# The down projection of a ConvFFN block: 16 of its 22 blocks of weights as seven products instead of eight

## The chip, the cores and the metric

The kernel runs on one core of a Trainium2 chip. The metric is the device time of the whole launch in microseconds. TensorE is PE in the profile (PEld is its loading of the stationary operand), VectorE is DVE, ScalarE is ACT, GpSimd is POOL and SyncE is SP.

## The reference

One decoder block on x of 512 tokens x 1024 channels, in float32. Two token mixers (a causal convolution and an HGRN2 recurrence) are merged by gates, projected, and added to the residual:

```
x = layer_norm(ALPHA * x + mix, ln1_g, ln1_b)
z = x @ w_ffn_in                                   # 1024 -> 2 * 2816
u, gv = split(z);  u = causal_dwconv(u, w_ffn_dw, b_ffn_dw)      # 3 taps
y_ffn = (gelu(u) * gv) @ w_ffn_out                 # 2816 -> 1024
x = layer_norm(ALPHA * x + y_ffn, ln2_g, ln2_b)
```

## The kernel before

Every product is made of three matmuls (mm3): both operands are split into a high part, the float32r cast, and a low part, the rest, and hi x hi, hi x lo and lo x hi are summed in PSUM. Weights lie in DRAM as tiles of 128 x 1024 floats (512 KB). `fetch(i)` loads one on SP's queue into a raw buffer (three of them), casts the high part on ScalarE and subtracts for the low part on VectorE; high and low parts have a ring of five buffers each. `weight(i)` fetches up to three tiles ahead.

The stages, in order: input projections and mixers (to about 400 us); the output projection with the first layer norm (437 to 482 us), whose result goes to DRAM as x1_d and, transposed and split, to x1h and x1l; the up projection; the down projection with the second layer norm.

The up projection has 22 blocks of 128 hidden channels. Blocks 0 to 2 are plain. Blocks 3 to 21 each replace eight half-size products by seven (`seven_up`, `seven`): `weight_sums` builds sums of quarters of a block's weights on VectorE, `factor_sums` once builds sums of the activations, and each block runs b11, b21, t1, t2, b22, t3 and then t4, which is held back as `pending` and runs inside the next block. `act` makes the hidden tile hT[j]. A block is 7 x 4 x 3 = 84 matmuls of 256 columns. Sums of the block ahead are prepared while a block runs.

The down projection is plain before: for 16 blocks, each weight tile is used for four token blocks and two column halves, so 24 matmuls of 512 columns for one tile; hidden(k) splits hT[k]. The last six blocks run token block by token block, so that the layer norm of one overlaps the matmuls of the next. In the first of the 16 blocks VectorE also multiplies x1a (the residual, read back from x1_d in one load of 2 MB) with the first layer norm's gain and adds its bias; gains and biases of both norms come as lnp, one broadcast load of 2 MB on POOL's queue.

The order within each engine's queue is made by a planner: it takes the program's order as priority, follows dependencies and buffers, and simulates with its own costs. A tile with the same tag as an older one takes that one's place once all its readers are done.

Of the kernel before, what the change touches and what calls it, by code (L numbers as in the profile page):

```python
# [13 lines left out]
PLAIN = 3  # L14
# [47 lines left out]


@with_exitstack
def hybrid_block(ctx: ExitStack, tc: tile.TileContext, wts: bass.AP, xT_d: bass.AP,
# [29 lines left out]
    def limit(i):  # L95
        return min(e for e in (W_G, W_FI + 2 * PLAIN, W_N) if e > i) - 1
# [14 lines left out]
    resident = {}  # L111

    def fetch(i):
        raw = wp.tile([P, 1024], F32, tag="raw", name=f"wr{i}", bufs=3)
        parts = 4 if i == 0 else 1
        n = 1024 // parts
        pieces = [slice(j * n, j * n + n) for j in range(parts)]
        for c in pieces:
            nc.sync.dma_start(raw[:, c], wts[i][:, c])
# [78 lines left out]

    pads = [p1p.tile([P, 64], F32, name="pad0")]
# [383 lines left out]
    def weight_sums(i, t, b21, extra):  # L583
# [210 lines left out]
    x1_d = ctx.enter_context(tc.tile_pool(name="dram", bufs=1, space=bass.MemoryType.DRAM)).tile([T, D], F32, name="x1_d")  # L794
# [28 lines left out]
    keep = {}  # L823

# [30 lines left out]
    for half in range(2):  # L855
# [22 lines left out]
    NK = 16  # L878
    hT = {}

    def hid():

        for tag, c0, n in [("ch", 0, 4), ("cl", 4, 4)] + [(f"sc{i}", 8 + 2 * i, 2) for i in range(4)]:
# [3 lines left out]
        for c in range(16, NFF):  # L887
            hT[c] = tmp.tile([P, T], F32, tag=("tot", "kt", "gg")[(c - 16) // 2], name=f"hT{c}")
# [40 lines left out]
    def prepare(j):  # L929
# [22 lines left out]
    hid()  # L952
# [16 lines left out]
    lnp = p1p.tile([P, 4, 1024], F32, tag="xl", name="lnp")  # L969
    po.dma_start(lnp, ln_d.unsqueeze(0).broadcast_to([P, 4, 1024]))  # L970
    bks = [4, 5, 0, 1, 2, 3, 6, 7]
    yps = {}

    res = p1p.tile([P, 4, 1024], F32R, tag="xh", name="fores")
    resident[W_FO + NK] = lambda: (res[:, 0], res[:, 1])
    resident[W_FO + NK + 1] = lambda: (res[:, 2], res[:, 3])
    x1a = p1p.tile([P, NT, 1024], F32, tag="ol", name="x1a")
    nc.sync.dma_start(x1a, x1_d.rearrange("(b p) c -> p b c", p=P))
    hres = [p1p.tile([P, 2, T], F32R, tag=f"sv{i}", name=f"hres{i}") for i in range(4)]
    hsp = {}  # L980

    def hidden(k):

        if k not in hsp:
            if NK <= k < NK + 4:
                hi, lo = hres[k - NK][:, 0], hres[k - NK][:, 1]
            else:
                if k % 2:
                    hl = tmp.tile([P, 2, T], F32R, tag="qq", name=f"hq{k}")
                    hi, lo = hl[:, 0], hl[:, 1]  # L990
                else:
                    hi, lo = [tmp.tile([P, T], F32R, tag=t, name=f"h{t}{k}") for t in ("kT", "t1")]
            split(hi, lo, hT[k])
            hsp[k] = (hi, lo)
        return hsp[k]
# [24 lines left out]
    ws = [weight(W_FO + k) for k in range(NK, NFF)]  # L1020
    for k in range(NK, NFF):
        hidden(k)
    for tb in range(NT):
        for n in range(2):
            for k in range(NK, NFF):
                down(k, ws[k - NK], tb, (n,))
# [4 lines left out]
        for n, c in enumerate(halves):  # L1031
            ve.scalar_tensor_tensor(x1a[:, tb, c], x1a[:, tb, c], ALPHA, yps[tb][n], ALU.mult, ALU.add)
# [9 lines left out]
def pack(inp):  # L1042
# [27 lines left out]
    tiles.append(f("w_ffn_out")[0].reshape(NFF, P, 1024))  # L1070
# [40 lines left out]
```

## Time and profile before

| | |
|---|---|
| Time, median of 3 runs | 840.9 us (840.44 to 841.75) |
| The profiled execution | 840.79 us, of which 839.0 us is the span of the trace |
| PE busy | 821.0 us, 98% |
| VectorE busy | 617.0 us, 74% |
| ScalarE busy | 460.6 us, 55% |
| DMA moved | 113.40 MB |

The span runs from the first to the last event of the trace on the core. PE's busy time is modelled, since matmuls overlap; whether PE waits is read from the chain of waits and from the start times of matmuls.

### The profile page before, as it was taken

What the parts mean: (1) busy time and instruction counts of PE and PEld (TensorE: products, weight loads), DVE (VectorE), ACT (ScalarE), POOL (GpSimd) and SP (SyncE); (2) the same over time, 40 slices, a digit from 0 to 9 for tenths busy, and PEclk for the clock granted to TensorE, in tenths of its full rate; (3) what the DMA queues carried; (4) which work ended last, traced back from release to release, by engine and by line L of the source; (5) the groups of instructions that cost most, each with busy time, mean ns of one, the idle gap of its engine ahead of it and who ended that gap; (6) DMA issues with size and microseconds to landing.
All of it is one profiled execution on the core that took longest, in us unless ns stands there. A gap on an engine that the chain in (4) does not pass through costs nothing.

```text
span 839.0 us, 14550 instructions
## 1 busy us (share of the span) xinstructions
PE 821.0 (98%) x5771; PEld 719.7 (86%) x5771; DVE 617.0 (74%) x1113; ACT 460.6 (55%) x820; POOL 87.8 (10%) x147
## 2 busy tenths in 40 slices
PE   8999999999999999999999999999999999999995
PEld 6888778777777778999978899999999999888884
DVE  5369999955587638788474689689998999844356
ACT  4455555667678865566641556566666666423200
POOL 0112431433332400000100000000000000000000
PEclk9999999999999999999999999999999999999998
DMA  8688666654543664233675332323333234634101
GB/s 287 177 180 206 167 148 155 166 135 128 130 126 98 170 171 138 76 104 110 162 242 187 115 113 76 95 84 104 118 106 101 101 102 161 271 121 130 46 26 75
DMA packets 32995, 113.40 MB, mean 135 GB/s; under 512 B 3616, under 2 KB 4512, under 8 KB 32800
## 3 DMA queue, kind: packets, MB, share of 16 engines
q1 hardware_dynamic: 24288, 82.85, 29.6%
q0 software_dynamic: 6480, 25.17, 14.9%
q10 hardware_dynamic: 2160, 4.47, 1.5%
q8 instruction: 45, 0.74, 0.4%
q14 instruction: 22, 0.18, 0.1%
HBM read 85.21 MB, written 4.19 MB: 107 GB/s over the span
## 4 chain that ended last, share of the span: by engine, by line
PE 78%; DVE 12%; ACT 4%; DMA 3%; issue 1%; DVEq 0%; ACTq 0%; POOLq 0%; SPq 0%
PE ps L159 25%; PE ps L160 24%; PE ps L161 24%; DVE cws L262 6%; DMA wr<-in_wts 2%; DMA xr<-in_xT 1%; PE ps L379 1%; ACT wh L127 1%; PE ps L528 1%; DVE tt L412 1%; PE ps L530 1%; PE ps L543 1%; DMA wl<-wr 1%; PE ps L517 1%; PE ps L492 0%
## 5 line engine op out<-in xcount | busy, mean ns | idle before, releaser
L159 PE MATMUL ps<-xh,wh 128*128 128x512 f32 x256 | 104.4, 409 | 0.5 <-ACT xh L152 0.4
L160 PE MATMUL ps<-xl,wh 128*128 128x512 f32 x256 | 100.9, 394 | 0.5 <-DVE xl L155 0.5
L161 PE MATMUL ps<-xh,wl 128*128 128x512 f32 x256 | 100.4, 392 | 0.0
L262 DVE SCALAR_TENSOR_TENSOR cws<-cws,par 128x512 f32<-128x512 f32 x120 | 84.8, 756 | 0.1
L140 ACT CAST wh<-wr 128x1024 fp32r<-128x1024 f32 x34 | 35.6, 1049 | 61.3 <-PE ps L161 34.3
L141 DVE TENSOR_TENSOR wl<-wr,wh 128x1024 fp32r<-128x1024 f32 (+1 forms) x38 | 43.2, 1139 | 34.7 <-ACT wh L140 34.4
L127 ACT CAST wh<-wr 128x1024 fp32r<-128x1024 f32 x44 | 46.4, 1057 | 39.1 <-PE ps L160 27.8
L159 PE MATMUL ps<-sh,shi_t 128*128 128x256 f32 x228 | 64.5, 283 | 0.0
L160 PE MATMUL ps<-sl,shi_t 128*128 128x256 f32 x228 | 64.5, 283 | 0.0
L161 PE MATMUL ps<-sh,slo_t 128*128 128x256 f32 x228 | 64.5, 283 | 0.0
L129 POOL DMA_DIRECT2D wl<-wr x44 | 38.6, 877 | 225.4 <-ACT wl L128 205.3
L159 PEld LDWEIGHTS ps<-xh,wh 128*128 128x128 f32 x256 | 48.2, 188 | 12.0 <-ACT xh L152 1.9
L161 PEld LDWEIGHTS ps<-xh,wl 128*128 128x128 f32 x256 | 48.1, 188 | 10.2
L160 PEld LDWEIGHTS ps<-xl,wh 128*128 128x128 f32 x256 | 48.2, 188 | 9.8 <-DVE xl L155 1.2
L155 DVE TENSOR_TENSOR slo_t<-Toh,shi_t 128x1024 fp32r<-128x1024 f32 x38 | 46.4, 1221 | 12.6 <-ACT shi_t L152 11.9
L152 ACT CAST shi_t<-Toh 128x1024 fp32r<-128x1024 f32 x38 | 39.9, 1050 | 16.7 <-PE ps L160 8.3
L128 ACT ACTIVATE wl<-wh 128x1024 fp32r<-128x1024 f32 x44 | 46.6, 1059 | 0.8
L159 PEld LDWEIGHTS ps<-sh,shi_t 128*128 128x128 f32 x228 | 43.8, 192 | 0.0
L160 PEld LDWEIGHTS ps<-sl,shi_t 128*128 128x128 f32 x228 | 43.8, 192 | 0.0
L161 PEld LDWEIGHTS ps<-sh,slo_t 128*128 128x128 f32 x228 | 43.8, 192 | 0.0
L568 ACT COPY pc<-ps 128x256 f32<-128x256 f32 x57 | 21.2, 372 | 37.0 <-PE ps L161 36.8
L155 DVE TENSOR_TENSOR slo_b<-wr,shi_b 128x1024 fp32r<-128x1024 f32 x27 | 32.9, 1218 | 2.4 <-ACT shi_b L152 2.4
(384 smaller groups left out, 2552.4 us busy)
## 6 DMA issues: line engine op xcount, KB each, us to landing
wr<-in_wts SPq DMA_DIRECT2D x141, 512.0 KB, 3.8
wl<-wr POOLq DMA_DIRECT2D x44, 512.0 KB, 4.9
xr<-in_xT ACTq DMA_DIRECT2D x8, 256.0 KB, 5.2
x<-in_x ACTq DMA_DIRECT2D x4, 512.0 KB, 9.9
x_d<-x SPq DMA_DIRECT2D x4, 512.0 KB, 4.1
x1a<-x_d SPq DMA_DIRECT2D x1, 2048.0 KB, 8.4
lnp<-in_ln POOLq DMA_DIRECT2D x1, 2048.0 KB, 10.6
out<-x1a SPq DMA_DIRECT2D x8, 256.0 KB, 2.0
```

The lines of the kernel that those rows point to most:

```text
L127: ac.copy(hi, raw)
L128: ac.mul(lo, hi, -1.0)
L129: po.dma_start(lo, raw, accum_op=ALU.add)
L140: ac.copy(hi[:, c], raw[:, c])
L141: ve.tensor_tensor(lo[:, c], raw[:, c], hi[:, c], ALU.subtract)
L152: ac.copy(hi, src)
L155: (lo_eng or ve).tensor_tensor(lo, src, hi, ALU.subtract)
L159: pe.matmul(ps, a[0], b[0], start=start, stop=False, skip_group_check=more)
L160: pe.matmul(ps, a[0], b[1], start=False, stop=False, skip_group_check=more)
L161: pe.matmul(ps, a[1], b[0], start=False, stop=stop, skip_group_check=more)
L262: ve.scalar_tensor_tensor(cacc[j], cpad[j][:, i:i + T], w, cacc[j], ALU.mult, ALU.add)
L568: f(*args)
```

## The change

The first 16 blocks of hidden channels (2048 of 2816) are treated as one 2 x 2 problem: tokens in halves of 256, hidden channels in halves of 1024, output columns in halves of 512. Seven products replace eight, in the order b11, t1, t2, b22, t3, b21, t4; each has four weight tiles of 128 x 1024 (two hidden blocks by 512 columns), repacked on the host. The operand of each product is made on VectorE from quarters of hT (`operand`): four sums for t1, t2, b22 and t3, and four splits for all seven.

The sums t1 to t4 of the weights are not built on VectorE. `fo_sums(j)` issues for blocks 4 to 19 of the up projection, on POOL's queue, a 64-byte store of a piece of hT[j-2] into the target (it holds the rest back until hT[j-2] exists), then a copy of 512 KB from DRAM to DRAM, then a DMA of 512 KB that accumulates into it. The down projection then loads 28 + 6 tiles instead of 22.

The products go into PSUM banks named X, W, Z and V, a pair of each. Four partial sums are read out into x1a between products (`take_sum`, after b11, t1, t2 and t3), and X and Z go on accumulating.

The first norm's gain and bias on the residual move from the down projection to the output projection (`residual`, for token blocks 0 and 1 among the second half's matmuls, for 2 and 3 after block 3 of the up projection has been prepared); the store to x1_d follows it. gb1 and gb2, two broadcast tiles each of 512 KB, replace lnp. x1a takes the place of x1l instead of that of the activation sums. The scratch tiles of `weight_sums` swap places with its spare ring entries (oh0, oh1 against oh2, oh3). There are four raw weight buffers instead of three; two pad tiles go and four convolution tiles get 64 floats shorter.

```diff
+FOP = ("b11", "t1", "t2", "b22", "t3", "b21", "t4")
+FO_OF = {"b11": 0, "b21": 4, "b22": 8, "b12": 12}
+NK = 16
+W_S = W_FO + 4 * len(FOP) + 6
...
+    tsum = {t: [dp.tile([P, 1024], F32, name=f"{t}_{m}") for m in range(4)] for t in ("t1", "t2", "t3", "t4")}
+
+    def source(i):
+        if i < W_FO:
+            return wts[i]
+        n = i - W_FO
+        if n >= 4 * len(FOP):
+            return wts[W_FO + NK + n - 4 * len(FOP)]
+        t, m = FOP[n // 4], n % 4
+        return wts[W_FO + FO_OF[t] + m] if t in FO_OF else tsum[t][m]
...
-        raw = wp.tile([P, 1024], F32, tag="raw", name=f"wr{i}", bufs=3)
+        raw = wp.tile([P, 1024], F32, tag="raw", name=f"wr{i}", bufs=4)
...
-    pads = [p1p.tile([P, 64], F32, name="pad0")]
...
-    cws = [p1p.tile([P, 1152], F32, tag=f"sc{j}", name=f"cws{j}") for j in range(4)]
+    cws = [p1p.tile([P, 1088], F32, tag=f"sc{j}", name=f"cws{j}") for j in range(4)]
...
+    gb1 = [p1p.tile([P, 1024], F32, tag=f"sc{2 + i}", name=f"gb1_{i}") for i in range(2)]
+    for i in range(2):
+        ac.dma_start(gb1[i], ln_d[i:i + 1].broadcast_to([P, 1024]))
+
+    def residual(tb):
+        ve.tensor_tensor(x1[tb], x1[tb], gb1[0], ALU.mult)
+        ve.tensor_tensor(x1[tb], x1[tb], gb1[1], ALU.add)
+        nc.sync.dma_start(x1_d[tb * P:tb * P + P, :], x1[tb])
...
-            nc.sync.dma_start(x1_d[tb * P:tb * P + P, :], x1[tb])
...
+            (late if half else steps).append(lambda tb=tb: residual(tb))
...
-        t = [p1p.tile([P, 1024], F32, tag=tag, name=f"T{tag}_{j}") for tag in ("oh2", "oh3")]
+        t = [p1p.tile([P, 1024], F32, tag=tag, name=f"T{tag}_{j}") for tag in ("oh0", "oh1")]
...
-        return weight_sums(i, t, b21, ("oh0", "oh1"))
+        return weight_sums(i, t, b21, ("oh2", "oh3"))
...
+    def fo_sums(j):
+
+        fo = lambda t, m: wts[W_FO + FO_OF[t] + m]
+        m, c = divmod(j - NF - 1, 4)
+        if 0 <= m < 4:
+            t, b, a = (("t1", "b12", fo("b11", m)), ("t3", "b12", fo("b22", m)), ("t2", "b22", tsum["t1"][m]),
+                       ("t4", "b21", tsum["t2"][m]))[c]
+
+            po.dma_start(tsum[t][m][0:1, 0:16], hT[j - 2][0:1, 0:16])
+            po.dma_start(tsum[t][m], fo(b, m))
+            po.dma_start(tsum[t][m], a, accum_op=ALU.add, max_dma_last_dim=4096)
+
     for j in range(NF, NFF):
+        fo_sums(j)
         if j == NF:
             w = prepare(j)
+            for f in late:
+                f()
+            hid(1)
...
-    lnp = p1p.tile([P, 4, 1024], F32, tag="xl", name="lnp")
-    po.dma_start(lnp, ln_d.unsqueeze(0).broadcast_to([P, 4, 1024]))
...
-    x1a = p1p.tile([P, NT, 1024], F32, tag="ol", name="x1a")
+    x1a = p1p.tile([P, NT, 1024], F32, tag="xl", name="x1a")
...
+    def operand(t):
+
+        out = []
+        for q in range(4):
+            g = lambda a: halfT[a, q]
+            if t == "t1":
+                src = s12[q]
+                ve.tensor_tensor(src, g("a21"), g("a22"), ALU.subtract)
...
+            else:
+                src = g({"b11": "a11", "b21": "a12", "t4": "a22"}[t])
+            o = homes[t][q](t)
+            split(o[:, 0], o[:, 1], src)
+            out.append((o[:, 0], o[:, 1]))
+        return out
+
+    C = {(i, n): None for i in range(2) for n in "XWZV"}
+    bks = dict(zip([(i, n) for n in "XWZV" for i in range(2)], [4, 5, 0, 1, 2, 3, 6, 7]))
+    into = {"b11": "X", "b21": "W", "t1": "Z", "t2": "X", "b22": "Z", "t3": "X", "t4": "X"}
...
+    ops = operand("b11")
+    for n, t in enumerate(FOP):
+        nxt = None
+        for m in range(4):
+            w = weight(W_FO + 4 * n + m)
+            if m == 1 and n + 1 < len(FOP):
+                nxt = operand(FOP[n + 1])
+            for c in range(2):
+                first, end = m == 0 and c == 0, m == 3 and c == 1
+                for i in range(2):
+                    if n == 0 and first:
+                        if i:
+                            pending.pop()()
+                        C[i, "X"] = bank(bks[i, "X"])
...
+                    mm3(C[i, into[t]], (hi, lo), (w[0][:, cs], w[1][:, cs]), new and first, end, not new)
+        for i in range(2):
+            take_sum(t, i)
+        ops = nxt
...
-    for k in range(NK):
-        if 2 <= k < 2 + NT:
-            x_ = x1a[:, k - 2]
-            ve.tensor_tensor(x_, x_, lnp[:, 0], ALU.mult)
-            ve.tensor_tensor(x_, x_, lnp[:, 1], ALU.add)
...
-        for tb in range(NT):
-            if k == 0:
-                if tb == 2:
-                    pending.pop()()
-                yps[tb] = [bank(bks[2 * tb + n]) for n in range(2)]
-            down(k, w, tb)
```

## Rows read from the trace of the kernel before

**Rows 1.** The page: the span, and each engine's busy time with its share of the span and its instructions.

```profile
span 839.0 us, 14550 instructions
PE 821.0 (98%) x5771; PEld 719.7 (86%) x5771; DVE 617.0 (74%) x1113; ACT 460.6 (55%) x820; POOL 87.8 (10%) x147
```

**Rows 2.** Busy time by stretch, us from the span's start: length, busy time and instructions of PE, PEld, DVE, ACT and POOL, then PE's granted clock as a share of full speed, DMA share and GB/s. The stretches are most of the output projection, the plain up blocks, up blocks 3 to 21, the down projection up to its last 144 matmuls, and the tail.

```profile
440.00:482.25 42.25, 42.25 (x195) 34.97 (x194) 22.42 (x41) 15.26 (x27) 0.00 (x0) 1.00 0.44 152
482.25:518.30 36.05, 36.05 (x303) 36.04 (x302) 33.09 (x63) 24.16 (x42) 0.00 (x0) 1.00 0.26 85
518.30:708.60 190.30, 190.30 (x1588) 190.30 (x1587) 170.10 (x219) 117.03 (x187) 0.00 (x0) 1.00 0.32 106
708.60:797.50 88.90, 88.90 (x400) 73.85 (x399) 47.69 (x53) 30.89 (x41) 0.56 (x1) 1.00 0.42 148
829.95:839.00 9.05, 0.00 (x0) 0.00 (x0) 5.47 (x14) 0.00 (x0) 0.00 (x0) 0.74 0.15 58
```

**Rows 3.** The chain of work that ended last, from 650 us on: its shares by engine and line, then two of its matmuls (start, length, line), each the last of a triple, with 25 triples from the one to the other.

```profile
by line: PE ps L161 31.8%; PE ps L160 31.7%; PE ps L159 31.7%; DVE x1a L1037 0.7%; DVE x1a L1038 0.4%; DVE lstb L1033 0.4%; DVE x1a L1032 0.4%; DVEq L1107 0.4%; DVE rst_b L172 0.3%; DVE lmvb L1034 0.1%; issue 0.1%; DVE rsq_b L180 0.1%; DVE 
...
737.92 0.23 PE ps L161
...
754.92 0.23 PE ps L161
```

**Rows 4.** Groups of instructions by line and shape, 680 to 839 us: line, engine, operation, names, shapes, count | busy us, mean ns of one | idle us before them and what ended it. A weight's subtraction, its cast, a split's subtraction, and a sum that reads PSUM.

```profile
L141 DVE TENSOR_TENSOR wl<-wr,wh 128x1024 fp32r<-128x1024 f32 x20 | 24.4, 1222 | 21.8 <-ACT wh L140 21.7
L140 ACT CAST wh<-wr 128x1024 fp32r<-128x1024 f32 x20 | 20.9, 1048 | 28.8 <-PE ps L161 20.2 <-issue 4.1 <-DMA wr<-in_wts 3.8
...
L1032 DVE SCALAR_TENSOR_TENSOR x1a<-x1a,ps 128x512 f32<-128x512 f32 x8 | 5.5, 684 | 13.9 <-PE ps L161 13.9
...
L155 DVE TENSOR_TENSOR ht<-hTsc,hkT 128x512 fp32r<-128x512 f32 x4 | 2.8, 691 | 7.7 <-ACT hkT L152 7.7
```

**Rows 5.** VectorE in order of time in the up projection: start, us, engine, line, operation.

```profile
601.26 0.68 DVE L155 TENSOR_TENSOR bt<-wr,bkT 128x512 fp32r<-128x512 f32 x1
601.87 0.69 DVE L605 TENSOR_TENSOR Toh<-wr,Toh 128x512 f32<-128x512 f32 x1
...
603.67 1.22 DVE L155 TENSOR_TENSOR slo_b<-wr,shi_b 128x1024 fp32r<-128x1024 f32 x1
604.81 2.52 DVE L155 TENSOR_TENSOR slo_t<-Toh,shi_t 128x1024 fp32r<-128x1024 f32 x2
```

**Rows 6.** PE in order of time: the last transposes of x1, the first matmul of up block 3, the first of the down projection, and the first of block 21's last product and of what follows it.

```profile
494.35 0.60 PE L828 MATMUL ps<-ident,x 128*128 128x128 f32 x4
...
518.54 0.28 PE L159 MATMUL ps<-x1h,shi_b 128*128 128x256 f32 x1
...
708.62 0.40 PE L159 MATMUL ps<-wh,hkT 128*128 128x512 f32 x1
...
711.37 0.28 PE L159 MATMUL ps<-x1h,shi_t 128*128 128x256 f32 x1
...
712.80 0.40 PE L159 MATMUL ps<-wh,hkT 128*128 128x512 f32 x1
```

**Rows 7.** The page's DMA issues: out<-in, queue, count, KB each, median us from issue to landing.

```profile
wr<-in_wts SPq DMA_DIRECT2D x141, 512.0 KB, 3.8
wl<-wr POOLq DMA_DIRECT2D x44, 512.0 KB, 4.9
...
x_d<-x SPq DMA_DIRECT2D x4, 512.0 KB, 4.1
x1a<-x_d SPq DMA_DIRECT2D x1, 2048.0 KB, 8.4
...
out<-x1a SPq DMA_DIRECT2D x8, 256.0 KB, 2.0
```

**Rows 8.** VectorE in order of time in the down projection; the bracket is the idle time before and what ended it.

```profile
723.73 2.36 DVE L1007 TENSOR_TENSOR x1a<-x1a,lnp 128x1024 f32<-128x1024 f32 x2 [3.38 <-DMA lnp<-in_ln]
```

**Rows 9.** DMA queues from 80 to 300 us: packets, MB, and the packets' time as a share of 16 engines over these 220 us. POOL's queue (q0) moved about 29 accumulates of 512 KB, SP's (q1) about 31 loads.

```profile
q0 software_dynamic: 4176, 15.21, 35.4%
q1 hardware_dynamic: 4464, 15.99, 22.0%
```

**Rows 10.** The waits of SP's queue ahead of the weight loads of the up projection, 560 to 700 us: count, then minimum, median and maximum in ns.

```profile
L590 SPq EVENT_SEMAPHORE  x25: 17/6167/9229, 554.1 to 675.1; - x25
```

**Rows 11.** Who PE waited for from 395 us on (longest in total): us in total, times, longest.

```profile
PE ps L159 <- DVE gm L776: 0.9, 1, 0.9
```

**Rows 12.** A POOL operation and a POOL DMA issue in order of time, VectorE in the same time, and the group from 80 to 300 us that the first of these VectorE operations belongs to.

```profile
106.98 1.73 POOL L365 TENSOR_TENSOR qq<-qq,tot 128x512 f32<-128x512 f32 x1 [1.09 <-DVE qq L364]
108.65 0.86 POOL L129 DMA_DIRECT2D wl<-wr  x1
...
107.48 1.24 DVE L412 TENSOR_TENSOR tt<-tt 128x4 f32<-128x4 f32 x1
108.65 2.06 DVE L262 SCALAR_TENSOR_TENSOR cws<-cws,par 128x512 f32<-128x512 f32 x3
...
L412 DVE TENSOR_TENSOR tt<-tt 128x4 f32<-128x4 f32 x8 | 2.4, 306 | 0.1
```

**Rows 13.** Busy time in the steady part of the up projection, columns as in rows 2.

```profile
560.00:700.00 140.00, 140.00 (x1169) 140.00 (x1169) 128.82 (x168) 88.15 (x139) 0.00 (x0) 1.00 0.32 106
```

**Rows 14.** VectorE in order of time: the split of block 4's b11.

```profile
517.94 1.21 DVE L155 TENSOR_TENSOR slo_b<-wr,shi_b 128x1024 fp32r<-128x1024 f32 x1
```

More of the change, by code (lines that the diff above doesn't have):

```diff
@@ L823, in hybrid_block @@
     keep = {}
+    late = []
     def ln1_transposes(half, tb, n):
@@ L886, in hid @@
                 hT[c0 + c] = t_[:, c]
-        for c in range(16, NFF):
+            for c in range(0, n, 2):
+                hT2.append(t_[:, c:c + 2])
+        for c in range(16, NFF) if part else ():
             hT[c] = tmp.tile([P, T], F32, tag=("tot", "kt", "gg")[(c - 16) // 2], name=f"hT{c}")
@@ L979, in hybrid_block @@
[L979 to L986, printed above, removed]
-            else:
[L988 to L995, printed above, removed]
@@ L997, in down @@
-    def down(k, w, tb, ns=(0, 1)):
-        hi, lo = hidden(k)
+    x1a = p1p.tile([P, NT, 1024], F32, tag="xl", name="x1a")
+    nc.sync.dma_start(x1a, x1_d.rearrange("(b p) c -> p b c", p=P))
+    gb2 = [tmp.tile([P, 1024], F32, tag="qq", name=f"gb2_{i}") for i in range(2)]
+    for i in range(2):
+        po.dma_start(gb2[i], ln_d[2 + i:3 + i].broadcast_to([P, 1024]))
+    halfT = {}
+    for q in range(4):
+        halfT["a11", q], halfT["a21", q] = hT2[q][:, :, 0:256], hT2[q][:, :, 256:512]
+        halfT["a12", q], halfT["a22", q] = hT2[4 + q][:, :, 0:256], hT2[4 + q][:, :, 256:512]
@@ new lines, in hybrid_block, with part, make @@
+    s12 = [tmp.tile([P, 2, 256], F32, tag="t1" if q < 2 else "t0", name=f"s12_{q}", bufs=2 if q < 2 else 3) for q in range(4)]
+    four = lambda *tags: [lambda k, t=t: p1p.tile([P, 2, 2, 256], F32R, tag=t, name=f"so{t}_{k}") for t in tags]
+    big = {}
+    def part(tag, q):
+        def make(k):
+            if q == 0:
+                big[tag] = p1p.tile([P, 4, 2, 2, 256], F32R, tag=tag, name=f"so{tag}_{k}")
+            return big[tag][:, q]
+        return make
+    homes = {"b11": four("at", "oh0", "oh1", "sv0"), "t1": [part("xh", q) for q in range(4)],
+             "t2": [part("ol", q) for q in range(4)], "b22": four("at", "oh0", "oh1", "sv0"),
+             "t3": four("sv1", "sv2", "sv3", "oh2"), "b21": [part("xh", q) for q in range(4)],
+             "t4": four("at", "oh0", "oh1", "sv0")}
@@ new lines, in operand @@
+    def operand(t):
+        out = []
+        for q in range(4):
+            g = lambda a: halfT[a, q]
+            if t == "t1":
+                src = s12[q]
+                ve.tensor_tensor(src, g("a21"), g("a22"), ALU.subtract)
+            elif t == "t2":
+                src = s12[q]
+                ve.tensor_tensor(src, src, g("a11"), ALU.subtract)
+            elif t == "b22":
+                src = s12[q]
+                ve.tensor_tensor(src, src, g("a12"), ALU.add)
+            elif t == "t3":
+                src = g("a21")
+                ve.tensor_tensor(src, g("a11"), src, ALU.subtract)
+            else:
+                src = g({"b11": "a11", "b21": "a12", "t4": "a22"}[t])
[3 more added lines that the diff above has]
+        return out
@@ new lines, in hybrid_block, with rows, take_sum @@
+    C = {(i, n): None for i in range(2) for n in "XWZV"}
+    bks = dict(zip([(i, n) for n in "XWZV" for i in range(2)], [4, 5, 0, 1, 2, 3, 6, 7]))
+    into = {"b11": "X", "b21": "W", "t1": "Z", "t2": "X", "b22": "Z", "t3": "X", "t4": "X"}
+    def rows(i, half, n):
+        return x1a[:, 2 * half + i, n * 512:n * 512 + 512]
+    def take_sum(t, i):
+        if t in ("b11", "t1", "t2"):
+            x_ = rows(i, *{"b11": (0, 0), "t1": (1, 1), "t2": (0, 1)}[t])
+            ve.scalar_tensor_tensor(x_, x_, ALPHA, C[i, into[t]], ALU.mult, ALU.subtract if t == "t2" else ALU.add)
+        elif t == "t3":
+            x_ = rows(i, 1, 1)
+            ve.tensor_tensor(x_, x_, C[i, "X"], ALU.subtract)
@@ new lines, in hybrid_block @@
+    ops = operand("b11")
[12 more added lines that the diff above has]
+                        C[i, "X"] = bank(bks[i, "X"])
+                    elif first and into[t] != "X" and C[i, into[t]] is None:
+                        C[i, into[t]] = bank(bks[i, into[t]])
+                    new = t in ("b11", "b21", "t1")
+                    hi, lo = (o[:, c, i * P:i * P + P] for o in ops[m])
+                    cs = slice(c * 512, c * 512 + 512)
+                    mm3(C[i, into[t]], (hi, lo), (w[0][:, cs], w[1][:, cs]), new and first, end, not new)
+        for i in range(2):
+            take_sum(t, i)
+        ops = nxt
@@ new lines, in hybrid_block @@
+    hres = p1p.tile([P, 4, 2, T], F32R, tag="ol", name="hres")
+    hid_ = []
+    for k in range(NK, NFF):
+        o = hres[:, k - NK] if k < NK + 4 else p1p.tile([P, 2, T], F32R, tag=("sv3", "oh2")[k - NK - 4], name=f"hres{k}")
+        split(o[:, 0], o[:, 1], hT[k])
+        hid_.append((o[:, 0], o[:, 1]))
+    resident[W_S - 1] = lambda: tuple(p1p.tile([P, 1024], F32R, tag=f"sv{1 + i}", name=f"fol{i}") for i in range(2))
+    ws = [weight(W_S - 6 + k) for k in range(6)]
+    for i in range(2):
+        C[i, "V"] = bank(bks[i, "V"])
@@ L1020, in hybrid_block @@
[L1020 to L1026, printed above, removed]
+            fresh = tb >= 2 and n == 1
+            for k in range(6):
+                mm3(yps[tb][n], (hid_[k][0][:, ts], hid_[k][1][:, ts]), (ws[k][0][:, c], ws[k][1][:, c]), fresh and k == 0,
+                    k == 5, not fresh)
         st = sml.tile([P, 2, 6], F32, tag="lst", name=f"lstb{tb}")
@@ L1069, in pack @@
     tiles.append(up)
-    tiles.append(f("w_ffn_out")[0].reshape(NFF, P, 1024))
+    wo = f("w_ffn_out")[0].reshape(NFF, P, 1024)
+    quad = lambda k, n: wo[k:k + 8, :, n * 512:n * 512 + 512].reshape(4, 2, P, 512).transpose(0, 2, 1, 3).reshape(4, P, 1024)
+    tiles += [quad(0, 0), quad(8, 0), quad(8, 1), quad(0, 1), wo[16:]]
     wts = np.ascontiguousarray(np.concatenate(tiles, 0))
```

43 lines of the change are left out of this document (17 added, 26 removed).

## The prediction

> **What bounds the kernel now.** I read the page first. TensorE (PE) is busy 821.0 of 839.0 us and VectorE (DVE) 617.0 [rows 1]. Such shares say little, so the second view is the busy time by stage [rows 2]: from 482.25 us to the last matmul at 829.95 PE is never idle, at a granted clock of 1.00, and after it comes a tail of 9.05 us on VectorE. VectorE runs 8.94 us of each 10.0 in the up projection (170.10 of 190.30) but only 47.69 of 88.90 in the part of the down projection that is changed. The third view, the chain that ended last, says the same by line: 95% of the last 189 us are the three matmuls of mm3 [rows 3]. So before the tail a matmul less is time won, as long as VectorE, ScalarE and the DMA queues can feed the rest faster than today. The change buys matmuls with VectorE work, so VectorE's rate is the question.
>
> **What the matmuls are worth.** In the chain the first of three matmuls of the down stage stands at 737.92 and the same one 25 triples later at 754.92 [rows 3]: 17.00/75 = 0.2267 us each (a profile's duration of one, 0.39, overlaps the next). Before, the down stage has 22 blocks x 4 token blocks x 2 halves x 3 = 528 of them, 119.7 us. After: seven products of 4 weights x 2 row blocks x 2 token blocks x 3 = 48 each, 336 for 16 blocks where 384 stood, and the last 6 blocks keep 144. 48 x 0.2267 = **-10.9 us**, if nothing waits. The shape is unchanged (128x128 loaded, 512 columns), so the price per matmul should hold.
>
> **VectorE in the down stage.** Durations are 1.22 us for a weight's subtraction (128x1024), 0.69 for a 128x512 split and 0.68 for a 128x512 sum that reads PSUM [rows 4], but back to back they start 1.14 and 0.61 apart [rows 5]. Weights are now 28 + 6 instead of 22. One of the products t1, t2, b22 or t3 needs, while its predecessor runs: 4 weights (4 x 1.14 = 4.56), four sums and four splits of the operand (8 x 0.61 = 4.88), and, except while t3 runs, two take_sum (1.22): 10.66 us, against 48 x 0.2267 = 10.88 of PE. That is 98%, with no room to catch up. b21 and t4 need no sums: 4.56 + 2.44 + at most 1.22 = 8.2. Removed from this stage are the eight 128x1024 operations on x1a (8 x 1.14 = 9.1).
> How much lead is there? The first down matmul is at 708.62, the last up product sits inside from 711.37 to 712.80 [rows 6], so b11 ends at 708.62 + 1.43 + 10.88 = 720.9. In those 12.3 us VectorE still has the end of blocks 20 and 21 (act and two sums: about eight operations at some 0.6, 4.8), two weights (2.3) and t1's operand (4.9): 12.0. The lead is a few tenths in program order, more if the planner takes weights first. I therefore charge **+1.1 us**, one weight subtraction that once comes late. The bounds: 0 if weights go first; above, if the operations cost their durations instead of their spacing, (4 x 1.22 + 10 x 0.69) - 10.88 = 0.9 on each of four products, 3.6. ScalarE casts the same eight tiles at 1.05 us or less [rows 4], at most 8.4 of 10.9, and is no bound.
>
> **x1a.** It moves from a buffer that came free at 708.8 to one that the last up product reads until 712.8 [rows 6], and took 8.4 us [rows 7]: 721.2, against its first use, take_sum of b11, at 720.9. Today VectorE sat 3.38 us until 723.73 there for the 2 MB of lnp [rows 8]; that load shrinks to two of 512 KB which only the tail uses. I take 0.3 us, inside the 1.1; if it lands only as late as lnp did, 723.7, 2.8 us. Weight loads queued behind it on SP have the fourth raw buffer: four weights of 2.72 us, 10.9, are on chip before x1a is issued. The sums X, Z and X that take_sum reads are written again one product (10.9 us) later, so the bank is no wait.
>
> **The sums in DRAM.** Blocks 4 to 19 get three POOL DMAs each: a 64-byte gate, a 512 KB copy, a 512 KB accumulate. No row shows DRAM to DRAM. Nearest rows: 2.0 us for a small store, 4.1 for 512 KB to DRAM, 4.9 for a 512 KB accumulate [rows 7]; a block lasts 10.0 us. The queue waits for gate and copy only, 6.1, plus three issues of 0.87 [rows 12], 8.7: it keeps pace with the blocks. On the 16 engines an accumulate cost 35.4% x 220/29 = 2.7 us and a load 22.0% x 220/31 = 1.6 [rows 9], so the up stage's share of 0.32 [rows 2] becomes about 0.32 + 4.3/10 = 0.75. Weight loads (3.8 us [rows 7]) may take some microseconds longer, but SP sat a median of 6.2 us for a free raw buffer before each issue [rows 10], and the fourth buffer lets the load start half a block (5 us) earlier. I take **0**. Without that cover: VectorE has 0.8 us of slack a block (128.82 of 140 busy, 9.2 of 10.0 [rows 13]), so loads that are 1 us late in each cost 0.2 x 16 = 3.
>
> **What moves ahead.** residual() puts four 128x1024 operations in the middle of the output projection and four behind it. The first go where VectorE idles today (22.4 of 42.25 us busy between 440 and 482.25 [rows 2]). The second fall where VectorE is full (33.1 of 36.05), and block 3's first product at 518.54 [rows 6] now needs buffers that come free only after them and their store: the last transpose that reads x1 starts at 494.35 [rows 6], then 2 x 2.3 of operations, 4.1 of store and 2.3 of split, 506 to 514 according to place. 4.6 us of VectorE time are charged to a lead of about one block, 10 us (b11 of block 4 was ready at 517.94 + 1.21 [rows 14] for a use at 518.54 + 10.0 = 528.5). **0**, above 4.6. gb1's load and three stores move with it, on ACT and SP while DMA is half idle: 0. The fourth raw buffer may shorten earlier waits; PE waits 0.9 us in all between 395 and the end [rows 11], so 0 to -0.9: 0. The tail keeps its operations: 0.
>
> **Sum.** 839.0 - 10.9 + 1.1 = 829.2; the profiled run was 840.79, 1.8 above its span, so **831.0 us**. The median, 840.9, is 0.1 above that run, which changes nothing. What can't be told from no change is 0.2%, 1.7 us.
>
> **Rivals.**
> *VectorE binds the heavy products* (or block 3's entry, or x1a): 98% by spacing speaks for it; against it, VectorE ran 33.1 of 36.05 us before block 3, and PE did not wait [rows 2], and b21 and t4 give 2.7 us each back to the queue, though not to PE. Time: 831.0 - 1.1 + 3.6 + a part of 2.8 and 4.6, that is 832.5 to 838 and a little above, 834.5 as its middle.
> *POOL's issues block VectorE in the up stage*: the one that ends slower. A POOL operation on SBUF does so today: while one ran from 106.98 to 108.71, a VectorE product of 128x4 took 1.24 us instead of 0.31 [rows 12]. Were a DMA issue of the same kind, three of 0.87 = 2.6 us a block against 0.8 us of slack would cost 1.8 x 16 = 29 us: 860. It decides from 0.8 + 10.9/16 = 1.5 us a block. Against it: in the 0.86 us issue at 108.65 three VectorE operations ran in 2.06, their usual 0.66 apart [rows 12]. [...]
> *The sums come late.* The fifteenth, t2's fourth, must have landed by 731.8 + 8.2 - 6.1 = 733.9 (t2's start, three weights of 2.72, a load of 3.8 with cast and subtraction) to load and split in time; from 528.5 that leaves 13.7 us a sum. At 16 it would be 35 us late: 866. Even 8.4, the 2 MB load's time, for the copy gives 2.0 + 8.4 + 0.9 = 11.3, so it is unlikely.
> *More is won*, below 828: early waits vanish, nothing slips.
>
> **Chances.** Forecast (828.5 to 832.5) 0.60; VectorE binds 0.25, of which 0.04 ends within 0.2% of before; more won 0.04; POOL blocks 0.07; late sums 0.04. Faster 0.60 + 0.21 + 0.04 = 0.85, same 0.04, slower 0.11. The range 828 to 838 takes in the first case and most of the second, and leaves out a little under 2 in 10.
>
> **What would show it.** 480 matmuls of 0.2267 us after about 708.6, the last near 820; DVE close to 10.7 of 10.9 in the products t1 to b22; x1a landing at 721; POOL's three issues each block of 10 us, with up-stage DVE operations at their old durations and PE still without idle time. Wrong would be: the up stage ending after 708.6, PE waiting on wl, on the operand's split or on a weight load from the sums, or block 3 starting after 518.5.

## The result, and the profile after

The changed kernel takes 829.74 us (median of 4 runs, 828.44 to 830.29), the kernel before 840.97 beside it; the ratio is 0.9864, 95% interval 0.9851 to 0.9876. The forecast was 831.0 in a range of 828 to 838. The profiled execution took 830.29 us, 1.8 above its span of 828.5. The head of its page, the span and the busy time of each engine, answers to [rows 1]:

```profile
span 828.5 us, 14682 instructions
PE 810.3 (98%) x5723; PEld 710.4 (86%) x5723; DVE 650.3 (78%) x1161; ACT 480.1 (58%) x844; POOL 117.2 (14%) x194
```

The span is 10.5 us shorter, PE has 10.7 less to do, and VectorE works 33 us more. Next, the busy time by stage: the first three lines are block 0 to block 3 of the up projection, the rest of the up projection, and the down projection up to the last six blocks. The columns are PE, PEld, DVE, ACT and POOL busy, the granted clock, the DMA share and GB/s.

```profile
481.73:518.01 36.28, 36.28 (x306) 36.28 (x304) 36.14 (x66) 24.41 (x43) 0.00 (x0) 1.00 0.23 82
518.01:708.09 190.08, 190.08 (x1587) 190.08 (x1586) 173.63 (x225) 117.48 (x188) 28.20 (x46) 1.00 0.68 187
708.09:786.00 77.91, 77.37 (x347) 63.79 (x346) 67.15 (x86) 47.69 (x63) 2.46 (x4) 1.00 0.76 248
...
719.80:730.70 10.90, 10.90 (x50) 9.03 (x49) 7.32 (x10) 3.98 (x5) 1.96 (x3) 1.00 1.02 322
730.70:742.20 11.50, 10.96 (x48) 8.74 (x48) 10.64 (x15) 8.91 (x14) 0.00 (x0) 1.00 0.64 218
742.20:753.10 10.90, 10.90 (x49) 9.03 (x49) 10.90 (x15) 9.25 (x14) 0.00 (x0) 1.00 0.64 198
753.10:764.00 10.90, 10.90 (x49) 9.02 (x49) 10.90 (x16) 7.76 (x10) 0.00 (x0) 1.00 0.75 241
```

What to see:
- **The up projection is as long as before** (36.28 + 190.08 us; from the starts 482.25, 518.54 and 708.62 of [rows 2, 6] before: 36.29 + 190.08), and PE is busy all of it, though the DMA share rose from 0.32 to 0.68 and POOL issues DMAs for 28 us.
- **The last four lines are the products t1, t2, b22 and t3** (by the starts of their first matmuls each begins 0.7 to 1.0 us after its line does). VectorE is full from 742.2 to 764.0, while b22 and t3 run, and PE does not wait for it. The forecast had worked out 10.66 of 10.88. But VectorE is not at its limit there, it works ahead: a weight's low part is finished 0.5 to 3.2 us before its first matmul in b22, and 3.5 to 4.6 us before it in t3.
- **While t1 runs the DMA engines are full** (1.02) and VectorE is not (7.32 of 10.90). Right behind it, in t2, stands the only loss of PE.

By the starts of the first and the last down matmul, that stretch took 120.94 us before and 111.01 after. 480 matmuls take 479 x 0.2267 + 1.43 (the last up product, which runs inside the stretch) = 110.0. So -10.9 came from the matmuls and about +1.0 was given back. Up to 708 the profiled run is 0.5 us ahead; that stretch's length is decided before 482 us, where the start of the up stage varied from 480.4 to 483.1 over the profiled runs of all kernels here, so I read nothing into it. The tail after the last matmul's start is 9.4 us in both.

The one visible loss, as all waits of PE from 380 us on (engine, line, what it waited for; us, times, longest):

```profile
PE ps L176 <- DVE gm L788: 0.6, 1, 0.6
PE ps L177 <- DVE wl L158: 0.5, 1, 0.5
```

The first lies in the output projection, as in [rows 11]. The second is at 735.08, in t2: the matmul starts 0.93 us after its forerunner instead of 0.23. The weight's low part (wl) came late. Why, VectorE's instructions show (start, duration, and in brackets idle time and what ended it):

```profile
721.94 1.28 DVE L1073 SCALAR_TENSOR_TENSOR x1a<-x1a,ps 128x512 f32<-128x512 f32 x2 [0.58 <-DMA x1a<-x_d]
724.27 2.42 DVE L158 TENSOR_TENSOR wl<-wr,wh 128x1024 fp32r<-128x1024 f32 x2 [1.05 <-ACT wh L157]
...
730.44 1.29 DVE L172 TENSOR_TENSOR sool_t<-s,sool_t 128x512 fp32r<-128x512 f32 x2 [1.95 <-ACT sool_t L169]
...
733.81 1.22 DVE L158 TENSOR_TENSOR wl<-wr,wh 128x1024 fp32r<-128x1024 f32 x1
```

VectorE stood idle four times here, 4.4 us in all (0.58, 1.05, 1.95, and 0.86 before the split at 733.20), and so lost its lead. ScalarE (next fence, waits from 690 to 828 us) waited for raw weights, which are the sums coming back from DRAM, and the casts for VectorE's splits stood behind them in its queue:

```profile
ACT wh L157 <- DMA wr<-t: 10.4, 6, 5.2
```

The chain that ended last passes through one of these loads, 10.06 us long. It was issued when VectorE's subtractions (the line above it) had freed a raw buffer:

```profile
719.08 2.28 DVE wl L158 x2
721.43 10.06 DMA wr<-t
731.59 1.05 ACT wh L157
733.81 1.23 DVE wl L158
```

What was under way there, as DMA issues from 700 to 780 us (KB each, median us from issue to landing):

```profile
wr<-t SPq DMA_DIRECT2D x16, 512.0 KB, 5.1
x1a<-x_d SPq DMA_DIRECT2D x1, 2048.0 KB, 11.0
t<-t POOLq DMA_DIRECT2D x2, 512.0 KB, 9.2
gb<-in_ln POOLq DMA_DIRECT2D x2, 512.0 KB, 11.9
```

x1a's 2 MB, issued at 710.85, landed at 721.9, 11.0 us later where [rows 7] had 8.4; the last copy and accumulate and gb2's 1 MB, which follows them on POOL's queue, were issued at 712.8, 720.25 and 720.8. So by this trace the slip comes from a crowd of transfers at the entry of the down projection, not from VectorE's work. Experiments 2 and 3 below test that, and experiment 9 limits it.

### The profile page after: what moved, and what is told of

Same layout as the page of the kernel before. It is cut to its first block, busy times and chain, and to the rows that moved or that the text cites. A ratio compares the mean times of both kernels' runs of the same rounds, so it can differ in the third digit from the quotient of the medians.

```text
span 828.5 us, 14682 instructions
## 1 busy us (share of the span) xinstructions
PE 810.3 (98%) x5723; PEld 710.4 (86%) x5723; DVE 650.3 (78%) x1161; ACT 480.1 (58%) x844; POOL 117.2 (14%) x194
## 4 chain that ended last, share of the span: by engine, by line
PE 77%; DVE 13%; ACT 5%; DMA 4%; issue 1%; DVEq 0%; ACTq 0%; SPq 0%
PE ps L176 24%; PE ps L177 24%; PE ps L178 24%; DVE cws L274 6%; DMA wr<-t 1%; DMA xr<-in_xT 1%; PE ps L391 1%; DMA wl<-wr 1%; PE ps L540 1%; PE ps L542 1%; ACT wh L144 1%; PE ps L529 1%; DVE tt L424 1%; DVE wl L158 1%; PE ps L555 1%
## 5 line engine op out<-in xcount | busy, mean ns | idle before, releaser
L157 ACT CAST wh<-wr 128x1024 fp32r<-128x1024 f32 x47 | 49.1, 1053 | 57.0 <-PE ps L178 31.5
L158 DVE TENSOR_TENSOR wl<-wr,wh 128x1024 fp32r<-128x1024 f32 (+1 forms) x51 | 58.6, 1161 | 15.7 <-ACT wh L157 15.6
L144 ACT CAST wh<-wr 128x1024 fp32r<-128x1024 f32 x44 | 46.5, 1059 | 38.9 <-PE ps L177 27.6
L172 DVE TENSOR_TENSOR slo_t<-Toh,shi_t 128x1024 fp32r<-128x1024 f32 x38 | 46.5, 1223 | 12.7 <-ACT shi_t L169 12.7
L169 ACT CAST shi_t<-Toh 128x1024 fp32r<-128x1024 f32 x38 | 39.5, 1048 | 14.8 <-PE ps L177 13.9
L172 DVE TENSOR_TENSOR slo_b<-wr,shi_b 128x1024 fp32r<-128x1024 f32 x27 | 33.0, 1223 | 2.4 <-ACT shi_b L169 2.4
## 6 DMA issues: line engine op xcount, KB each, us to landing
x<-in_x ACTq DMA_DIRECT2D x4, 512.0 KB, 10.1
```

The lines of the kernel that those rows point to most:

```text
L169: ac.copy(hi, src)
L172: (lo_eng or ve).tensor_tensor(lo, src, hi, ALU.subtract)
```

## The experiments

Theory: the matmuls saved set the time, VectorE's queue at 98% with a small lead is the next limit, the DRAM sums are hidden, and the fourth raw buffer is their cover. The rivals are those of the prediction. Ratios are to the kernel before on the same chip; runs within about 1 us of each other can't be told apart by their medians, so small effects are read from the stretch between the first and last down matmul (111.01 us in the changed kernel). Such a stretch is that of one profiled execution.

**1. Only the fourth raw buffer** (the kernel before; cws narrower and the pads out, for room).

```diff
-tag="raw", name=f"wr{i}", bufs=3
+tag="raw", name=f"wr{i}", bufs=4
-    pads = [p1p.tile([P, 64], F32, name="pad0")]
```

> The kernel before with a fourth raw weight buffer alone, and the room made for it (two pad tiles gone, convolution tiles 64 floats shorter). Theory, that the gain is 48 matmuls and the buffer only shortens waits ahead of the down projection (whose first matmul stood at 708.62 before and 708.09 after): 840.97 - 0.5 = 840.4. Rival, that the buffer and the layout carry a large part of the 11.2 us: 836 or less.

839.75 us, ratio 0.9982 (0.9973 to 0.9991). Down stretch 120.94, as before. Alone the buffer is worth about 1.5 us (0.0018 x 841), a little more than the bound of 0.9. By the traces it does not lie behind the start of the up projection: from there to the first down matmul both kernels take 226.4 us, then 120.94, and the tails differ by 0.1. It can only lie ahead of it (480.77 here, 482.25 before), in a part whose length varies by 2.7 us over the profiled runs; what it shortens there isn't settled.

**2. The changed kernel without its sums** (the products load plain weight tiles in their place).

```diff
-        fo_sums(j)
-        return wts[W_FO + FO_OF[t] + m] if t in FO_OF else tsum[t][m]
+        return wts[W_FO + FO_OF.get(t, 12) + m]
```

> The changed kernel without the sums in DRAM: no gate, copy or accumulate on POOL's queue, and the products t1 to t4 load the plain tiles of b12 in their place, so the work of the sums is left out and their loads stay. Theory, that the sums are hidden except where the last two meet x1a's load (PE waited 0.93 us between two starts at 734.15 and 735.08): 829.7 - 0.7 = 829.0. Rival, that they cost nothing: 829.7. Rival, that 0.68 instead of 0.32 of DMA share slows the whole up projection: 826 or less.

830.15 us, ratio 0.9867 (0.9854 to 0.9881): the sums' 48 DMAs cost nothing that the time shows. In the trace the wait in t2 is gone and the down stretch is 110.17, 0.15 from the ideal. The stretches of t1 and t2 by busy time:

```profile
719.80:730.70 10.90, 10.90 (x50) 9.03 (x49) 9.55 (x13) 5.49 (x7) 0.00 (x0) 1.00 0.92 350
730.70:742.20 11.50, 11.50 (x53) 9.52 (x52) 11.40 (x17) 9.22 (x15) 0.00 (x0) 1.00 0.59 183
```

VectorE has done 9.55 us of work in the first line, where it had done 7.32: what had kept its weights away is gone. That is the last sum's copy and accumulate, but not these alone: with POOL's queue free, gb2's two loads were issued at 712.95 and 718.94 instead of 720.8 and 721.4. This run does not separate the two.

**3. The sums issued in pairs**, every second block two gates, then two copies, then two accumulates, so that fewer of them stand behind an accumulate. (Shortened; `two` holds the sums of this block and the next.)

```diff
-        if 0 <= m < 4:
+        if 0 <= m < 4 and c % 2 == 0:
+            for t, b, a in two: po.dma_start(tsum[t][m][0:1, 0:16], hT[j - 2][0:1, 0:16])
+            for t, b, a in two: po.dma_start(tsum[t][m], fo(b, m))
+            for t, b, a in two: po.dma_start(tsum[t][m], a, accum_op=ALU.add, max_dma_last_dim=4096)
```

> The changed kernel with the sums issued in pairs: every second block two gates, then two copies, then two accumulates, the same 48 transfers. Today the chain needs 11.8 us where a block has 10.0, because a gate issued 0.55 us after an accumulate lands 6.3 us later; so the last accumulate goes out at 720.3, beside x1a. In pairs the last should go out near 700. Theory, that the wait of PE at 735 comes from that crowd: it goes, 829.7 - 0.7 = 829.0. Rival, that VectorE's full queue made it: 829.7.

829.92 us, ratio 0.9866 (0.9853 to 0.9879). The last accumulate is issued at 688.6 instead of 720.25, PE has no wait at all in the down stage, and the stretch is 110.15. With the sums in but out of the entry, the slip is gone too (and gb2 is out earlier again, at 711.23 and 717.25). Its 0.9 us stand in the trace and are too small for the medians.

**4. VectorE loaded further**: one more 128x512 operation for each quarter of the operands of t1, t2, b22 and t3.

```diff
+            if t in ("t1", "t2", "b22", "t3"):
+                ve.tensor_tensor(src, src, src, ALU.max)
```

> The changed kernel with one more VectorE operation of 128x512 (a maximum with itself, which changes no value) for each of the four operand pieces of t1, t2, b22 and t3. Theory, that VectorE is full in these products (10.66 of 10.88 us): 10.66 + 4 x 0.61 = 13.1, so 2.2 too much in each of four, 8.9, less a lead of about 1.5: 837. Rival, that VectorE has room there and only the DMA made PE wait: under 831.

838.0 us, ratio 0.9968 (0.9955 to 0.9981), 8.3 more than without. But not all of it is VectorE's. Busy time in slices of 1 us, columns as above:

```profile
731.00:732.00 1.00, 0.00 (x0) 0.00 (x0) 0.20 (x1) 0.00 (x0) 0.00 (x0) 1.00 1.02 418
732.00:733.00 1.00, 0.00 (x0) 0.00 (x0) 0.00 (x0) 0.91 (x1) 0.00 (x0) 1.00 0.93 381
...
734.00:735.00 1.00, 1.00 (x3) 0.51 (x3) 0.98 (x2) 0.37 (x1) 0.00 (x0) 0.52 0.07 29
735.00:736.00 1.00, 1.00 (x4) 0.79 (x3) 0.00 (x0) 1.00 (x2) 0.00 (x0) 0.50 0.02 8
736.00:737.00 1.00, 1.00 (x4) 0.81 (x3) 0.77 (x2) 1.00 (x3) 0.00 (x0) 0.50 0.00 0
```

PE waits 3.1 us up to 733.71 with VectorE idle and the DMA engines full, and then runs at a granted clock of 0.50. The crowd of the entry is in it again, so that the 837 I expected was met by the number and not by its reason.

**5. The same load with the sums in pairs** takes the crowd away (the edits of 3 and 4 together).

> e3's extra VectorE operation (2.44 us in each of t1, t2, b22 and t3) together with the pairs of e7, so without the crowd of transfers in which e3 lost most (PE waited 3.1 us at 730.6 and then ran 3.5 us at half clock). Theory, that VectorE is full by itself: 8.9 less a lead of 1.5 to 4, so 834.5 to 837. Rival, that e3's loss was the crowd: under 832.

833.12 us, ratio 0.9906 (0.9889 to 0.9923), between the theory's 834.5 and the rival's 832; down stretch 113.28, that is 3.1 over experiment 3's. The load is 16 x 0.61 = 9.8 us of VectorE [rows 5]. By the forecast's count 4 x 0.22 = 0.9 of it fit into the products' slack; of the other 8.9 only 3.1 were paid, so 5.8 us were taken up elsewhere, where the forecast saw a lead of a few tenths. In experiment 3, without the load, the trace shows that lead: a weight's low part is finished at least 3.3 us before its first matmul in t1, 2.2 in t2, 2.5 in b22 and 5.5 in t3; in the changed kernel it is 0.05 at the wait in t2. Besides, half of t3's operand is made ahead (two sums and two splits, the last at 711.50 in the changed kernel), which the count charges to the time of b22. Of the 8.3 us of experiment 4, more than half was the crowd and the clock.

**6. Three raw buffers in the changed kernel.**

```diff
-bufs=4)
+bufs=3)
```

> The changed kernel with three raw weight buffers again. Theory, that the fourth covers the entry of the down projection, where weight loads took 8.4 us (median) beside x1a's 2 MB and the last sums: a weight is loaded one place later, 2.7 us, so PE waits about 2.7 there, and the 0.5 of the earlier stages are lost too: 833. Rival, that a raw buffer is worth 0.5 wherever it is: 830.2.

843.24 us (841.02 to 850.11 in 10 runs), ratio 1.0029 (1.001 to 1.0048): the whole gain is lost, where I expected 3 us. The profiled execution is the slowest of the ten, so its trace tells where, not how much. PE's longest waits from 470 us on:

```profile
PE ps L176 <- ACT pc L580: 6.6, 5, 2.6
PE ps L176 <- ACT fol L157: 1.3, 1, 1.3
```

The weight loads of up blocks 3 to 21 (line 602; us to landing, least, median, most) and ScalarE's wait for them (us, times, longest), first of this kernel, then of the changed kernel:

```profile
DMA to landing us min/median/max: 3.4/5.8/9.1
ACT bkT L169 <- DMA wr<-in_wts: 40.3, 16, 5.6
```

```profile
DMA to landing us min/median/max: 3.4/4.3/8.6
ACT bkT L169 <- DMA wr<-in_wts: 0.7, 1, 0.7
```

The up projection took 200.98 us after block 3's start instead of 190.08, and the down stretch 118.34. Loads land later, and with one buffer less they are also issued later. PE's longest waits are for a copy of a partial sum out of PSUM (pc) on ScalarE, whose queue stood before it at a cast that waited for a raw weight.

**7. Three raw buffers and no sums** (edits 6 and 2 together).

> Three raw buffers as in e6 (843.2), and no sums in DRAM as in e2 (the work of the sums is left out, t1 to t4 load plain tiles of b12). It asks why three buffers lost 10.9 us in up blocks 3 to 21 and 7.3 in the down projection. Theory, that the sums' transfers delay the weight loads (5.8 us to landing in e6, 4.3 with four buffers, 3.8 before) and three buffers leave no time for that: without the sums the up blocks take 190.1 us again and only part of the 7.3 stays: 831 to 834. Rival, that the buffers' new places in blocks 3 to 21, or three buffers for 34 tiles, are enough: 840 or more.

832.77 us, ratio 0.9910 (0.9892 to 0.9929); up projection 190.09. With experiments 2 and 6 that makes a square: the third-to-fourth buffer is worth 13.5 us with the sums (843.24 - 829.74) and 2.6 without (832.77 - 830.15). The four were measured on different chips; by the ratios it is 13.9 and 3.6. The sums' traffic is what three buffers can't bear.

**8. Sums made late**: the copy issued twice.

```diff
             po.dma_start(tsum[t][m], fo(b, m))
+            po.dma_start(tsum[t][m], fo(b, m))
```

> The changed kernel with the copy of each sum made twice, one after the other, which lengthens POOL's chain and nothing else. The chain is 11.8 us a sum now (152.9 us for 13), so 11.8 + 4.6 + 0.5 = 16.9. Theory, that a sum must not take more than 13.7: the fifteenth (t2's fourth) lands at 521 + 15 x 16.9 + 7 = 781, where 734 is needed, 47 us late: about 876. Rival, that there is far more room than that: 829.7 to 831.

860.92 us, ratio 1.0233 (1.0214 to 1.0251). Late sums cost time, 15 us less than expected. PE's instructions that waited longest, the first in t1, the second in t2:

```profile
736.93 0.80 PE L176 MATMUL ps<-wh,soxh_t 128*128 128x512 f32 x1 [8.06 <-ACT wh L157]
...
764.92 0.79 PE L176 MATMUL ps<-wh,sool_t 128*128 128x512 f32 x1 [13.81 <-ACT wh L157]
```

The first accumulate was issued at 533.65, the fifteenth at 754.53: 15.8 us a sum, against the 13.7 from which lateness was to count and the 16.9 that I had expected; 1.1 us in each of fourteen intervals are the 15. After both waits PE's matmuls started 0.43 us apart instead of 0.23, until 742.20 and 769.33, which is in the price too.

**9. Another order of products**, with b21 ahead of t3, so that the bank of X is used by two products in a row.

```diff
-FOP = ("b11", "t1", "t2", "b22", "t3", "b21", "t4")
+FOP = ("b11", "t1", "t2", "b22", "b21", "t3", "t4")
```

> The changed kernel with b21 before t3, so that t3 and t4 write the banks X one right after the other and take_sum of t3 has to read them in between. Theory, that the order by banks hides that read: PE waits about 0.9 us (one 128x512 read of 0.61 and a semaphore): 829.7 + 0.9 = 830.6. Rival, that it makes no difference, or that b21 among the heavy products gives VectorE a rest and helps: 829.7 or less.

829.49 us, ratio 0.9874 (0.9852 to 0.9896). PE waits 0.4 us once for the read-out into x1a. That the order spares the banks is worth 0.4 us, below what the time can show.

This run shows something else. Up to b22 its program is that of the changed kernel, and its sums were even later: the last accumulate was issued at 727.84 and gb2 at 728.40, some 7.6 us later than there. Yet PE has no wait in t2. The weights loaded meanwhile (issued at 720.0 to 726.2) landed in 4.6 to 7.3 us, not in 8.4 to 10.1, and VectorE was 2.1 us ahead at the place of the wait. So late sums at the entry do not always cost the 0.9 us; by these two traces it depends on which weights the last accumulate and gb2 meet.

**10 and 11. Can the entry be made lighter?** Both have the pairs of experiment 3 and x1a in the place of t2's operand (t2 and hres take x1a's). In the first, gb2 goes to a buffer that is free after b21; in the second, to two that are free after t4. (Shortened.)

```diff
-    x1a = p1p.tile([P, NT, 1024], F32, tag="xl", name="x1a")
+    x1a = p1p.tile([P, NT, 1024], F32, tag="ol", name="x1a")
-    gb2 = [tmp.tile([P, 1024], F32, tag="qq", name=f"gb2_{i}") for i in range(2)]
+    gbt = p1p.tile([P, 2, 1024], F32, tag="xh", name="gb2")       # 10
+    gb2 = [p1p.tile([P, 1024], F32, tag=t, name=f"gb2_{t}") for t in ("at", "oh0")]   # 11
```

> The pairs, and two more loads taken out of the crowd at the entry of the down projection: gb2 goes into xh, which comes free after b21's product (about 764 us), and x1a goes into ol, which comes free 2.5 us earlier than xl (t2's operand and the last hidden tiles change to xl). Theory: no wait of PE in the down projection is left, which would be 829.7 - 1.0 = 828.7. Rival, VectorE's full queue: 829.7.

> The pairs, x1a in ol, and gb2 in places that come free after t4 (at and oh0, about 785 us), so that its 1 MB meets neither the entry nor the last six weights, where the version with gb2 at 774 made PE wait 1.4 us. Theory: the down projection's 480 matmuls take 110.1 us from the first start to the last, as in e7 (110.15), and the time is that of e7 within 0.2%, 829.5; what is left to win there is nothing. Rival: the earlier x1a wins or loses 1 us more.

830.3 us, ratio 0.9879 (0.9861 to 0.9897), down stretch 112.20; and 830.04 us, 0.9873 (0.9859 to 0.9888), 111.08. In the first, gb2's 1 MB was issued at 774.40 and met the raw weights of the last six blocks:

```profile
785.00:790.00 5.00, 3.54 (x15) 2.39 (x14) 2.36 (x2) 1.99 (x2) 0.00 (x0) 1.00 0.01 2
```

PE idles 1.46 us with nothing on the DMA engines any more: the two weights issued beside gb2 landed in 8.4 and 6.9 us instead of 3.4 to 3.6. In the second, gb2 went out at 778.32 and 781.03, the last weight beside it took 5.8 us, and PE waited 0.63 us for it at 789.48, so the 110.1 I expected was missed as well. No wait is left at the entry in either, but gb2, moved, costs as much elsewhere, while in experiment 3 PE has no wait at all. No version here beats the changed kernel by more than can be measured.

## Why the prediction was right, and where its steps were not

**The matmuls: right.** 48 x 0.2267 was the term that set the time; the spacing of matmuls did not change, and the stretch came out within 0.2 us of 110.0 wherever PE did not wait (experiments 2, 3).

**The slip of +1.1: right in size by luck, wrong in cause.** I charged "one weight subtraction that once comes late", and one did (0.54 us of named wait, 0.7 by the starts). But it was to come late because VectorE had a lead of "a few tenths" and no room; in fact VectorE is 2.2 us ahead or more in t1 to t3 where nothing crowds the entry (experiment 3), and the subtraction came late since ScalarE and VectorE had stood waiting for raw weights. With sums that were later still there was no slip (experiment 9), so its size is a matter of which transfers happened to meet. The step that failed is the account of the lead in program order: it did not see that half of t3's operand is made ahead, and left out of the sum that x1a, the last sum and gb2 share the DMA engines with the weights there.

**The fourth raw buffer: set at 0, worth about 1.5 us** (experiment 1, 0.8 to 2.3 by its interval), where 0.9 had been the bound. That is the size of what is left between the forecast, 831.0, and the result, 829.74; that it is worth the same in the changed kernel is argued, not shown.

**x1a: right, but by two misses.** 721.2 was worked out as 712.8 + 8.4, and 721.9 measured as 710.85 + 11.0: it was issued earlier and took longer. 0.58 us of VectorE's wait, not on PE's path.

**The sums "keep pace with the blocks": wrong, without cost.** POOL's instructions (gate, copy, accumulate on lines 989 to 991; idle time and releaser in brackets):

```profile
544.40 0.49 POOL L990 DMA_DIRECT2D t<-in_wts  x1 [2.78 <-DMA t<-hTch]
549.05 0.85 POOL L991 DMA_DIRECT2D t<-in_wts  x1 [4.16 <-DMA t<-in_wts]
...
634.37 0.85 POOL L991 DMA_DIRECT2D t<-in_wts  x1 [3.47 <-DMA t<-in_wts]
634.93 0.80 POOL L989 DMA_DIRECT2D t<-hTsc  x1
641.50 0.49 POOL L990 DMA_DIRECT2D t<-in_wts  x1 [5.77 <-DMA t<-hTsc]
...
703.48 0.80 POOL L989 DMA_DIRECT2D t<-hT  x1
712.81 0.49 POOL L990 DMA_DIRECT2D t<-in_wts  x1 [8.53 <-DMA t<-hT]
```

The wait for the copy is 4.16 and 3.47 us in these lines, near the 4.1 I took. The gate isn't 2.0: with no accumulate under way the wait for it is 2.78 in the first line, and 5.77 where it is issued 0.55 us behind one. In all thirteen cases of that kind its 64 bytes landed 0.2 to 0.8 us after the 512 KB in front of them. From the gate at 550.59 to that at 703.48 13 sums take 11.76 us each, where I had 8.7 and a block takes 10.0. Each sum falls 1.8 us further behind; the sixteenth was issued at 720.25 and ran into the entry. The chain stayed under 13.7, so nothing came late, and experiment 8 shows the price above it. The DMA share of the stage, 0.75 in the forecast, was 0.68.

**The cover: named rightly, priced wrongly.** The forecast set 0 because of the fourth buffer and the free time on SP, and 3 us without them. With the buffer it is 0 (experiment 2); without it 10.5 us for the sums (843.24 - 832.77). The term 0.2 x 16 took loads to be 1 us late and VectorE to pay only what exceeds its slack. In experiment 6 the loads land 1.5 us later in the median (5.8 against 4.3), but they are also issued later, and PE's largest wait there is for ScalarE, which stood 40.3 us at loads, not for VectorE, whose slack I had counted. In the profiled execution the granted clock fell as well, to 0.50 in the slices of 547 and 548 us. How the 10.5 us (10.0 by the ratios) divide between later issue, longer landing and clock stays open.

**The moved residual: right at 0.** From block 0's start to block 3's start are 36.28 us, 36.29 before; VectorE is busy 36.14 of them, so what was hidden is hidden with little to spare.

**The rivals.** VectorE as the bound: busy all of b22 and t3 (10.90 of 10.90), but ahead of PE, and the one wait for it goes with the crowd (experiments 2, 3). Its price was also added up wrongly: 831.0 - 1.1 + 3.6 is 833.5, not the 832.5 at which its range began. POOL's issues blocking VectorE: false. VectorE's 128x1024 subtraction in the up stage has a mean of 1.22 us in both kernels (1223 ns after, 1221 ns before), while POOL issues DMAs for 28.20 us of that stage:

```profile
L172 DVE TENSOR_TENSOR slo_t<-Toh,shi_t 128x1024 fp32r<-128x1024 f32 x38 | 46.5, 1223 | 12.7 <-ACT shi_t L169 12.7
```

```profile
L155 DVE TENSOR_TENSOR slo_t<-Toh,shi_t 128x1024 fp32r<-128x1024 f32 x38 | 46.4, 1221 | 12.6 <-ACT shi_t L152 11.9
```

Of the 54 operations of this shape on line 172 in blocks 3 to 21, the 23 that overlapped an issue took 1.22 us each, as the other 31 did. Beside the POOL product of [rows 12] a VectorE operation took 1.24 us instead of 0.31; beside the DMA issues nothing like it shows. Sums late: false here, true in experiment 8.

## What to carry to other kernels

Seven products for eight were worth the matmuls saved, times their spacing (48 x 0.2267 = 10.9 us); VectorE, counted at 98% of a product, was enough since it entered with some microseconds in hand (3.3 to 7.5 in t1). Background DMA traffic was free only with the deeper prefetch (no cost that the time shows with four raw buffers, 10.5 us with three): change the depth and the traffic together, and price each with the other present. Look at the place where a new stage begins: here its first transfers came together (DMA share 1.02 while t1 ran), and moving one hit another place (experiments 10 and 11) or none (experiment 3).

## What was not expected of the hardware

After PE had idled 3.10 us (experiment 4, to 733.71) its granted clock was 1.00 in the slice of 733 us, 0.52 in that of 734, 0.50 in the next two, 0.77 in that of 737 and 1.00 in that of 738. After 2.60 us of idling in experiment 6 (to 545.40) it was 1.00 in the slice of 545, 0.70 in that of 546, 0.59 in that of 549 and 1.00 in that of 550. Three of its slices:

```profile
544.00:545.00 1.00, 0.00 (x0) 0.00 (x0) 1.00 (x3) 0.62 (x2) 0.00 (x0) 1.00 0.00 0
...
547.00:548.00 1.00, 1.00 (x7) 1.00 (x7) 1.00 (x2) 1.00 (x3) 0.00 (x0) 0.50 0.36 45
548.00:549.00 1.00, 1.00 (x6) 1.00 (x6) 1.00 (x1) 0.31 (x2) 0.00 (x0) 0.50 1.08 160
```

So these two waits cost more than themselves: the slow matmuls that followed them (0.43 us apart instead of 0.23 in experiment 4, 0.21 instead of 0.12 in experiment 6) count too. Later in experiment 6 matmuls of 512 columns started 0.43 us apart from 809.57 to 812.56 and 0.23 apart after 812.83. Other waits stood in stretches whose clock reads 1.00: 0.54 us in the changed kernel (730.70 to 742.20), 1.27 in experiment 4 (738 to 741), 1.7 in experiment 5 (741 to 752), 0.51 and 0.95 in experiment 10 (785 to 790). A second point is the gate: a 64-byte DMA had a median landing of 6.3 us in the changed kernel, nearly that of the accumulates of 512 KB, 6.7, behind which most of them stood; the two gates there with no accumulate under way, issued at 521.00 and 541.12, landed in 3.7 and 2.8 us.
